# A decoder layer with 32 experts: the experts' last 32 slots on 512-wide column tiles, their later steps moved in the order

## The chip, the core and the metric

The kernel runs on one core of one Trainium2 chip. The metric is the device time of one execution in microseconds (us); the kernel before took 2203.43 us, the median of three runs (2196.72 to 2205.83). TensorE (PE) multiplies, VectorE (DVE) and ScalarE (ACT) work elementwise, GpSimd (POOL) issues the indirect transfers, and SyncE (SP) issues the loads of the weights. Each engine takes its instructions strictly in the order in which they stand in its program; only semaphores tie the engines together.

## The reference

One layer on 2048 tokens of width 1024, in float32: a mixer (gated linear attention beside dilated attention), then a hierarchical mixture of experts, then a norm. The change is in the experts alone:

```python
def hier_moe(n, w_grp, b_grp, w_exp, b_exp, w1, w3, w2):
    # top-1 group of 8 experts, then the top 2 experts in it; their gates
    gate = jax.nn.softmax(top_v, axis=-1) * g_prob
    ...
    def expert_block(args):
        toks, e = args
        xb = x[toks]
        hb = jax.nn.silu(xb @ w1[e]) * (xb @ w3[e])
        return hb @ w2[e]
    y = lax.map(expert_block, (row_tok.reshape(n_blk, MOE_BLOCK), blk_exp))
    y = y.reshape(R, D).astype(jnp.float32) * row_w[:, None]
    out = jnp.zeros((M, D), jnp.float32).at[row_tok].add(y)
```

There are 32 experts. `w1` and `w3` of an expert are 1024 x 512, `w2` is 512 x 1024. On average an expert gets 128 of the 4096 chosen places.

## The kernel before, in words

The program runs in stages: projections and linear attention, attention, output projection and router, and from about 1310 us on the experts, one after another (`moe`). A table made by the router gives each expert 160 slots. Slots 0 to 127 are an expert's **first rows**, slots 128 to 159 its **last 32 slots**. An overflow loop behind the experts takes what is left.

**Weights.** Each expert has six pieces of 1 MB, in the order w1a, w3a, w1b, w3b, w2a, w2b (L1319 to L1330). SyncE loads a piece into one of six buffers (`raw`), so a piece takes the buffer that the same piece of the expert before had, and its load waits until all readers of that one are done. ACT rounds it (`hi`), DVE subtracts (`lo`); the first rows use `hi` and `lo` in three products each, the last 32 slots read `raw` itself. So `raw` of w1 and w3 is free when the last 32 slots' first products have read it, and `raw` of w2 when their second products have.

**First rows of an expert.** U: 48 products of 128 x 512 (L1379 to L1381). Then `h` = silu times gate on ACT and DVE (L1393, L1394). X: four transposes (L1406). ACT and DVE copy them as `hh` and `hl` (L1409). D: 24 products with w2 (L1428 to L1430). ACT and DVE evict `y`, POOL adds it to the result in DRAM (L1436). T: eight transposes of the next expert's tokens (L1354) and their copies `nh` and `nl` (L1357).

**The last 32 slots.** Four products of 32 columns of the array stand beside each other, one on each quarter of it ("pack"). u: 32 products of 256 columns for w1 and w3 (L1388); `hr` = silu times gate (L1399, L1400); x: two transposes (L1414) and a copy `ht` (L1416); d: 16 products of 256 columns with w2 (L1444); one eviction `yr` (L1447) and an add (L1448).

**What sets the order.** The code records operations; a scheduler with its own costs then places each engine's instructions, so pieces of u stand between the products of U where it expected a wait. `behind` (NoSync) sets an order without a wait. `order` (called after expert 1) computes where every token's result goes, POOL scatters it in 16 transfers (L1251), and a load of `places` (L1256) reads it back on SyncE's queue. `entries` (called before expert 0) loads the table and computes the row numbers `i4` of the last slots' quarters on DVE (L1238 to L1240).

Of the kernel before, what the change touches and what calls it, by code (L numbers as in the profile page):

```python
# [60 lines left out]
class Layer:  # L61
# [1144 lines left out]
    def moe(self):  # L1206
        tc, nc, a = self.tc, self.nc, self.a
        with self.moest as st:
# [8 lines left out]
            rps = pool("e_rps", 2, space=PSUM)  # L1217
            acc4 = self.acc.rearrange("t (g c) -> (t g) c", g=4)
# [3 lines left out]
            i4A = keep.tile([128, NE], I32, name="i4")  # L1222
# [23 lines left out]
            def order():  # L1246
# [103 lines left out]

            def turn(G):
                tp = tps.tile([128, KD, 128], F32, name="tp")
                for k in range(KD):
                    nc.tensor.transpose(tp[:, k, :], G[:, k * 128:(k + 1) * 128], self.ident)  # L1354
# [13 lines left out]
            def up(w, x, nr=None):  # L1368
# [25 lines left out]
                nc.vector.tensor_tensor(to(h), by(ps[1]), to(h), OP.mult)  # L1394
                hr = None
                if nr is not None:
                    hr = gp.tile([128, 256], F32, name="hr", bufs=1)
                    by, to = (lambda t: t.rearrange("t (p k) -> t k p", k=2)), hr[64:128].rearrange("t (k p) -> t k p", k=2)
                    nc.scalar.activation(to, by(pr[0:64]), AF.Silu)  # L1399
                    nc.vector.tensor_tensor(to, by(pr[64:128]), to, OP.mult)  # L1400
                return h, hr

            def across(h, hr):
                tp = mm.tile([128, 4, 128], F32, name="mm")
                for k in range(4):
                    nc.tensor.transpose(tp[:, k, :], h[:, k * 128:(k + 1) * 128], self.ident)  # L1406
# [3 lines left out]
                ht = None  # L1410
                if hr is not None:
                    tr = rps.tile([128, 2, 64], F32, name="r")
                    for c in range(2):
                        nc.tensor.transpose(tr[:, c, :], hr[64:128, c * 128:(c + 1) * 128], self.ident[64:128, 64:128])  # L1414
                    ht = gp.tile([128, 2, 2, 32], F32, name="ht", bufs=1)
                    nc.vector.tensor_copy(ht, tr.rearrange("p c (u s) -> p u c s", u=2))  # L1416
                return hh, hl, ht

            def down(w2, x, it, irs, e=None):
                hh, hl, ht = x  # L1420
                y = yp.tile([128, D], F32, name="y", bufs=1)
                gate = it[:, 1:2].bitcast(F32)
                for f in range(2):
                    py = mm.tile([128, 512], F32, name="mm")
                    fs = slice(f * 512, (f + 1) * 512)
                    for k in range(4):
                        raw, hi, lo = w2[k // 2]
                        nc.tensor.matmul(py, hh[:, k, :], hi[:, k % 2, fs], start=k == 0, stop=False)  # L1428
# [4 lines left out]
                    else:  # L1433
# [3 lines left out]
                                                   in_=y, in_offset=None, compute_op=OP.add), e)  # L1437
                if ht is not None:
                    ir, i4 = irs
                    pr = rps.tile([128, 256], F32, name="r")  # L1440
# [7 lines left out]
                    added(nc.gpsimd.indirect_dma_start(out=acc4, out_offset=bass.IndirectOffsetOnAxis(ap=i4, axis=0),  # L1448
                                                       in_=yr, in_offset=None, compute_op=OP.add), e)
# [15 lines left out]
            for e in range(NE):  # L1465
# [7 lines left out]
                if e % 4 == 0 and e + 2 < NE:  # L1473
                    R = gather_last(e // 4, min(4, NE - 2 - e))
                h = across(*up((w1, w3), x, nr[:, :, at:at + 32]))
                at += 32
                if e + 1 < NE:
                    x = turn(G.pop(e + 1))
                    if e % 4 == 1:
                        nr, at = turn_last(R, 32 * min(4, NE - 1 - e)), 0  # L1480
                    for t, c in zip(self.turned, self.crossed):
                        self.behind(t, c, "what the tensor engine waits for comes first")
                if e == 0:
                    self.firstst.close()
                    yp = pool("e_y", 1)
                if e == NE - 1:

                    done = [(j, x, scale(x, self.crossed)) for j, x, _ in blocks]
                    for d in done[0:2]:
                        give(*d, after=(self.crossed[1],))  # L1490
                down(w2, h, itA[:, e], (irA[:, e], i4A[:, e:e + 1]), e)
                if waiting:
# [14 lines left out]
            with tc.For_i(0, n, 1) as i:  # L1507
# [10 lines left out]
                x = turn(gx)  # L1518
                down(w2, across(*up((w1, w3), x)), it, None)
                m = nc.values_load(cur[:, 2:3], min_val=0, max_val=NT)  # L1520
# [96 lines left out]
```

## Time and profile before

| What | Value |
|---|---|
| median of three runs | 2203.43 us |
| the profiled execution | 2199.59 us, its span 2197.6 us |
| mean granted TensorE clock over the span | 0.971 |
| PE busy, DVE, ACT, POOL | 2081.0, 1273.2, 1057.4, 529.7 us |
| experts, first X to last X | 1341.2 to 2153.7 us |
| DMA, HBM read and written | 342.46 MB and 92.08 MB |

A row of a timeline gives start, duration, engine, line, operation, `out<-in` and shape; instructions of one group that follow each other are merged (x64 is 64 records; a float32 product of u or d leaves two records). In brackets stands the idle time of the engine before the row, and what ended it. A busy PE counts records that overlap, so the distance between starts is what a product costs.

### The profile page before, as it was taken

To read this page: it belongs to the slowest core of one execution; us is meant where nothing else is said; L and a number is where in the kernel's file an instruction comes from. 1 tells how busy PE (TensorE), PEld (TensorE's weight loads), DVE (VectorE), ACT (ScalarE), POOL (GpSimd) and SP (SyncE) were. 2 spreads that over 40 slices of the span, in tenths; PEclk is the share of its full clock that TensorE was granted. 3 is DMA by queue.
4 is the path that set the end of the run, shared out by engine and by line. 5 is a ranking of instruction groups with operands and counts; after the bars stand their busy time and mean duration, and the time that the engine had idled before them with its cause. 6 is when DMAs were issued, how large, how long until landed. Compare 5 with 4: busy or idle time off the path is not lost. (4 is left out here: it accounts for less than half of the span.)

```text
span 2197.6 us, 38549 instructions
## 1 busy us (share of the span) xinstructions
PE 2081.0 (95%) x15258; PEld 1564.8 (71%) x15258; DVE 1273.2 (58%) x2481; ACT 1057.4 (48%) x1813; POOL 529.7 (24%) x370
## 2 busy tenths in 40 slices
PE   7999999999997999999989968999999999999993
PEld 7799889899885766666667755667677666667662
DVE  5203346334444556666645875767777677776773
ACT  5412336433322367767723443555555555565652
POOL 2000001000002001432421243622232254333334
PEclk9999999999998999999989979999999999999997
DMA  8333333233325624552457836788888889898974
GB/s 253 107 125 106 114 113 121 96 110 123 105 87 171 199 75 125 152 135 81 115 161 254 272 129 209 265 290 302 303 305 295 284 304 354 309 340 290 345 280 140
DMA packets 189000, 436.56 MB, mean 199 GB/s; under 512 B 35025, under 2 KB 106498, under 8 KB 162946
## 3 DMA queue, kind: packets, MB, share of 16 engines
q1 hardware_dynamic: 139090, 347.65, 44.9%
q0 software_dynamic: 21488, 60.36, 10.3%
q10 hardware_dynamic: 28240, 26.07, 4.0%
q8 instruction: 121, 1.98, 0.4%
q14 instruction: 61, 0.50, 0.1%
HBM read 342.46 MB, written 92.08 MB: 198 GB/s over the span
## 5 line engine op out<-in xcount | busy, mean ns | idle before, releaser
L1329 DVE TENSOR_TENSOR lo<-raw,hi 128x2048 fp32r<-128x2048 f32 x192 | 438.5, 2290 | 122.5 <-ACT hi L1329 121.3
L1329 ACT CAST hi<-raw 128x2048 fp32r<-128x2048 f32 x192 | 365.0, 1905 | 194.7 <-DMA raw<-expert_w 163.1
L588 ACT ACTIVATE P<-P,st 128x256 f32<-128x256 f32 (+1 forms) x384 | 174.0, 455 | 96.6 <-DVE st L586 92.2
L1381 PE MATMUL mm<-lo,nh 128*128 128x512 f32 x512 | 206.2, 404 | 0.7 <-DVE lo L1329 0.7
L1379 PE MATMUL mm<-hi,nh 128*128 128x512 f32 x512 | 204.4, 400 | 1.3 <-ACT nh L1357 1.3
L1380 PE MATMUL mm<-hi,nl 128*128 128x512 f32 x512 | 201.4, 393 | 0.0
L131 POOL TENSOR_TENSOR ss<-ss,mhalf 128x1 f32<-128x1 f32 (+1 forms) x32 | 28.9, 903 | 692.9 <-DVE ss L130 691.4
L217 PE MATMUL mm<-whi,nh 128*128 128x256 f32 x640 | 182.3, 285 | 0.0
L218 PE MATMUL mm<-wlo,nh 128*128 128x256 f32 x640 | 180.6, 282 | 0.0
L219 PE MATMUL mm<-whi,nl 128*128 128x256 f32 x640 | 179.5, 280 | 0.0
L586 DVE CUSTOM_DVE_ANT_0 P<-s,amask 128x256 f32<-128x256 f32 (+1 forms) x384 | 125.0, 362 | 66.4 <-PE s L582 42.9
L194 PE MATMUL mm<-nh,whi 128*128 128x512 f32 x384 | 155.3, 404 | 0.0
L195 PE MATMUL mm<-nl,whi 128*128 128x512 f32 x384 | 153.8, 400 | 0.0
L196 PE MATMUL mm<-nh,wlo 128*128 128x512 f32 x384 | 152.7, 398 | 0.0
L1388 PE MATMUL r<-raw,nr 128*32 128x256 f32 x2048 | 147.1, 383 | 0.0
L582 PE MATMUL s<-k,q 64*128 64x256 f32 (+1 forms) x768 | 132.8, 416 | 0.4 <-DVE st L586 0.4
L1381 PEld LDWEIGHTS mm<-lo,nh 128*128 128x128 f32 x512 | 96.6, 189 | 41.0 <-issue 17.3
L1436 POOL DMA_INDIRECT acc<-y,it x32 | 84.7, 2647 | 155.9 <-ACT y L1432 147.0
L185 DVE TENSOR_TENSOR wlo<-raw,whi 128x1024 fp32r<-128x1024 f32 (+1 forms) x48 | 57.1, 1227 | 111.4 <-ACT whi L184 111.4
L217 PEld LDWEIGHTS mm<-whi,nh 128*128 128x128 f32 x640 | 120.0, 188 | 2.0 <-issue 0.7
L219 PEld LDWEIGHTS mm<-whi,nl 128*128 128x128 f32 x640 | 121.1, 189 | 0.1
L218 PEld LDWEIGHTS mm<-wlo,nh 128*128 128x128 f32 x640 | 120.3, 188 | 0.1
(352 smaller groups left out, 4412.3 us busy)
## 6 DMA issues: line engine op xcount, KB each, us to landing
raw<-expert_w SPq DMA_DIRECT2D x192, 1024.0 KB, 9.6
raw<-w_in ACTq DMA_DIRECT2D x48, 512.0 KB, 5.0
fb<-fac SPq DMA_DIRECT2D x24, 384.0 KB, 7.7
x<-x SPq DMA_DIRECT2D x16, 512.0 KB, 6.2
og<-og SPq DMA_DIRECT2D x32, 256.0 KB, 2.9
xr<-x SPq DMA_DIRECT2D x32, 256.0 KB, 3.0
v<-av SPq DMA_DIRECT2D x8, 1024.0 KB, 7.9
hp<-xr SPq DMA_DIRECT2D x32, 256.0 KB, 2.2
```

The lines of the kernel that those rows point to most:

```text
L194: nc.tensor.matmul(ps, hi[:, k, ms], nh[q][:, k, :], start=k == 0, stop=False)
L195: nc.tensor.matmul(ps, hi[:, k, ms], nl[q][:, k, :], start=False, stop=False)
L196: nc.tensor.matmul(ps, lo[:, k, ms], nh[q][:, k, :], start=False, stop=k == KD - 1)
L217: nc.tensor.matmul(ps[:, j, :], h, hi[:, k, :], start=j == 0 and k == 0, stop=False, skip_group_check=True)
L218: nc.tensor.matmul(ps[:, j, :], h, lo[:, k, :], start=False, stop=False, skip_group_check=True)
L219: nc.tensor.matmul(ps[:, j, :], l, hi[:, k, :], start=False, stop=k == KD - 1, skip_group_check=True)
L588: nc.scalar.activation(P[:, h, 0:w], P[:, h, 0:w], AF.Exp, bias=nm, scale=-1.0, accum_out=dn)
L1329: split = nc.scalar.copy(hi, raw), nc.vector.tensor_tensor(lo, raw, hi.bitcast(F32), OP.subtract)
L1379: nc.tensor.matmul(ps[m], nh[:, k, :], hi[:, kk, :], start=k == 0, stop=False)
L1380: nc.tensor.matmul(ps[m], nl[:, k, :], hi[:, kk, :], start=False, stop=False)
L1381: nc.tensor.matmul(ps[m], nh[:, k, :], lo[:, kk, :], start=False, stop=k == KD - 1)
L1388: nc.tensor.matmul(pr[32 * g:32 * g + 32], nr[:, k, :], raw[:, k % 4, (g % 2) * 256:(g % 2) * 256 + 256], start=k == 0, stop=k == KD - 1, ...
```

## The change

Five things change; the code around them stays.

- u and d use 512-wide products, half as many: two quarters of the array take w1 and w3 of one part of the contraction, the other two those of another part. Their results are halves of a sum that must be added: ACT copies one half and DVE adds the other (`sm`), silu and gate follow on 32 x 512 (`sg`, `hr`); after d, ACT scales one half and DVE adds the other (`yr`). Row numbers are now of half rows (`i2`).
- `gated` is recorded after T and its copies, and is put behind them on ACT and DVE (`self.ahead`).
- x is recorded inside the second half of D instead of before D, d stays behind D.
- T is put behind X (`turn(..., self.inner)`).
- The row numbers of the last slots are computed behind `hl` of expert 0 (`rows`), and the load of `places` comes after expert 4 (`order_late`).

```diff
@@ entries, order
-                f4 = gp.tile([128, NE], F32, name="f4", bufs=1)
-                nc.vector.tensor_copy(f4[:, es], irA[:, es, 0])
-                nc.vector.tensor_scalar(f4[:, es], f4[:, es], 4.0, self.gcol, OP.mult, OP.add)
-                nc.vector.tensor_copy(i4A[:, es], f4[:, es])
+            def rows(es):
+
+                f2 = gp.tile([64, NE], F32, name="f2", bufs=1)
+                self.behind(nc.vector.tensor_copy(f2[:, es], irA[0:64, es, 0]), self.crossed[1], "the table's entries come later than the first inner values")
...
+                return free, sts
+
+            def order_late(free, sts):
                 l = nc.sync.dma_start(places, self.perm.rearrange("(p j) c -> p (j c)", p=128))
@@ up
-                    pr = rps.tile([128, 256], F32, name="r")
-                    for k in range(KD):
+                    pr = rps.tile([128, 512], F32, name="r")
+                    for k in range(0, KD, 2):
                         for g in range(4):
-                            raw = w[g // 2][k // 4][0]
-                            nc.tensor.matmul(pr[32 * g:32 * g + 32], nr[:, k, :], raw[:, k % 4, (g % 2) * 256:(g % 2) * 256 + 256],
-                                             start=k == 0, stop=k == KD - 1, skip_group_check=True, tile_position=(0, 32 * g))
+                            kk, raw = k + g // 2, w[g % 2][k // 4][0]
+                            nc.tensor.matmul(pr[32 * g:32 * g + 32], nr[:, kk, :], raw[:, kk % 4, :],
+                                             start=k == 0, stop=k == KD - 2, skip_group_check=True, tile_position=(0, 32 * g))
...
+            def gated(pr):
+
+                hr = gp.tile([128, 256], F32, name="hr", bufs=1)
+                sm = gp.tile([64, 512], F32, name="sm", bufs=1)
+                sg = gp.tile([64, 512], F32, name="sg", bufs=1)
+                first = nc.scalar.copy(sm, pr[64:128]), nc.vector.tensor_tensor(sm, pr[0:64], sm, OP.add)
+                for f, t in zip(first, self.ahead):
+                    self.behind(f, t, "the wide products come first")
+                act = nc.scalar.activation(sg[32:64], sm[0:32], AF.Silu)
+                by = lambda t, u: t[:, 256 * u:256 * u + 256].rearrange("t (p k) -> t k p", k=2)
+                for u in range(2):
+                    to = hr[64 + 32 * u:96 + 32 * u].rearrange("t (k p) -> t k p", k=2)
+                    vec = nc.vector.tensor_tensor(to, by(sm[32:64], u), by(sg[32:64], u), OP.mult)
+                self.gated = act, vec
+                return hr
@@ down
+                        if f and k == 2 and hr is not None:
+                            ht = across_last(hr)
...
-                    for k in range(4):
+                    for k in range(0, 4, 2):
...
-                            nc.tensor.matmul(pr[32 * g:32 * g + 32], ht[:, k // 2, k % 2, :], raw[:, k % 2, g * 256:g * 256 + 256],
-                                             start=k == 0, stop=k == 3, skip_group_check=True, tile_position=(0, 32 * g))
-                    yr = yp.tile([128, 256], F32, name="yr", bufs=1)
-                    nc.vector.tensor_scalar(yr, pr, ir[:, 1:2].bitcast(F32), None, OP.mult)
+                            kk, f = g // 2, g % 2
+                            nc.tensor.matmul(pr[32 * g:32 * g + 32], ht[:, k // 2, kk, :], raw[:, kk, f * 512:f * 512 + 512],
+                                             start=k == 0, stop=k == 2, skip_group_check=True, tile_position=(0, 32 * g))
+                    yr = yp.tile([64, 512], F32, name="yr", bufs=1)
+                    nc.scalar.activation(yr, pr[64:128], AF.Copy, scale=ir[64:128, 1:2].bitcast(F32))
+                    nc.vector.scalar_tensor_tensor(yr, pr[0:64], ir[0:64, 1:2].bitcast(F32), yr, op0=OP.mult, op1=OP.add)
@@ the loop over the experts
-                h = across(*up((w1, w3), x, nr[:, :, at:at + 32]))
+                h, pr = up((w1, w3), x, nr[:, :, at:at + 32])
+                h = across(h)
                 at += 32
+                self.ahead = self.crossed
                 if e + 1 < NE:
-                    x = turn(G.pop(e + 1))
+                    x = turn(G.pop(e + 1), self.inner)
...
+                    rows(slice(0, NE))
...
+                hr = gated(pr)
...
-                down(w2, h, itA[:, e], (irA[:, e], i4A[:, e:e + 1]), e)
+                down(w2, h, itA[:, e], hr, (irA[:, e], i2A[:, e:e + 1]), e)
...
-                    order()
+                    ordered = order()
+                if e == 4:
+                    order_late(*ordered)
```

What the scheduler makes of it is read from the built programs. First TensorE around the second pack (d), a middle expert of the kernel before: T, x, D, d, then the next expert's U, with u in three pieces between its products and X at the end.

```order
L1354 MATMUL tp<-ident,G 128x128 x8
L1414 MATMUL r<-ident,hr 128x64 x2
L1428 MATMUL mm<-hi,hh 128x512 x2
...
L1444 MATMUL r<-raw,ht 32x256 x16
L1379 MATMUL mm<-hi,nh 128x512
...
L1388 MATMUL r<-raw,nr 32x256 x5
...
L1388 MATMUL r<-raw,nr 32x256 x23
L1406 MATMUL mm<-ident,h 128x128 x4
```

The same stretch of a middle expert of the changed kernel: D (L1449 to L1451) is followed by U of the next expert (L1386 to L1388), and x (L1433) and d (L1466) stand between those products.

```order
L1359 MATMUL tp<-ident,G 128x128 x8
L1449 MATMUL mm<-hi,hh 128x512 x2
...
L1386 MATMUL mm<-hi,nh 128x512
...
L1433 MATMUL r<-ident,hr 128x64 x2
...
L1466 MATMUL r<-raw,ht 32x512 x8
L1396 MATMUL r<-raw,nr 32x512 x16
L1424 MATMUL mm<-ident,h 128x128 x4
```

x has left the place between T and D, and d has moved from the end of D to behind all 48 of the next expert's U, just ahead of u and X.

Then DVE at expert 0 before (`nr` is the copy of the last slots' transposed tokens, `f` and `i` the row numbers, `lo` a piece's subtraction):

```order
L1365 COPY nr<-tp 128x8x64
L1238 CAST f_13075<-ir 128x32
L1239 TENSOR_SCALAR f_13075<-f_13075,kcol 128x32
L1329 TENSOR_TENSOR lo<-raw,hi 128x2048
L1240 CAST i_13038<-f_13075 128x32
L1394 TENSOR_TENSOR h<-mm,h 128x512
```

and in the changed kernel:

```order
L1372 COPY nr<-tp 128x8x64
L1334 TENSOR_TENSOR lo<-raw,hi 128x2048
L1402 TENSOR_TENSOR h<-mm,h 128x512
L1427 TENSOR_TENSOR hl<-mm,hh 128x512
L1240 CAST f_13207<-ir 64x32
L1241 TENSOR_SCALAR f_13207<-f_13207,kcol 64x32
L1242 CAST i_13038<-f_13207 64x32
```

The row numbers, which read the table's entries, now stand behind `h` and `hl` of expert 0.

## Rows read from the trace of the kernel before

**Rows 1.** The page's busy line: engine, us, share of the span, instructions.
```profile
PE 2081.0 (95%) x15258; PEld 1564.8 (71%) x15258; DVE 1273.2 (58%) x2481; ACT 1057.4 (48%) x1813; POOL 529.7 (24%) x370
```
**Rows 2.** Window over the experts: us, busy (x) PE, PEld, DVE, ACT, POOL, PEclk, DMA, GB/s.
```profile
1450.00:2150.00 700.00, 692.45 (x4967) 482.96 (x4960) 501.30 (x380) 401.89 (x319) 241.69 (x117) 1.00 0.87 308
```
**Rows 3.** Timeline of PE, the first X (expert 0) and the last (expert 31).
```profile
1341.20 1.12 PE L1406 MATMUL mm<-ident,h 128*128 128x128 f32 x4 [7.97 <-DVE h L1394]
...
2153.65 0.66 PE L1406 MATMUL mm<-ident,h 128*128 128x128 f32 x4
```
**Rows 4.** Timeline of PE, one expert's turn: start us, us, engine, line.
```profile
1809.59 3.66 PE L1388 MATMUL r<-raw,nr 128*32 128x256 f32 x64
1813.18 0.65 PE L1406 MATMUL mm<-ident,h 128*128 128x128 f32 x4
1813.67 1.04 PE L1354 MATMUL tp<-ident,G 128*128 128x128 f32 x8
1814.64 0.33 PE L1414 MATMUL r<-ident,hr 64*128 64x64 f32 x2
1814.90 0.73 PE L1428 MATMUL mm<-hi,hh 128*128 128x512 f32 x2
...
1820.68 1.93 PE L1444 MATMUL r<-raw,ht 128*32 128x256 f32 x32
```
**Rows 5.** Timeline of PE, a piece of u between two products of U.
```profile
1826.35 0.39 PE L1379 MATMUL mm<-hi,nh 128*128 128x512 f32 x1
1826.57 0.39 PE L1380 MATMUL mm<-hi,nl 128*128 128x512 f32 x1
1826.89 1.05 PE L1388 MATMUL r<-raw,nr 128*32 128x256 f32 x10
1827.87 0.50 PE L1381 MATMUL mm<-lo,nh 128*128 128x512 f32 x1
```
**Rows 6.** Waits of SyncE's queue, 1450 to 2150 us: total us, times, longest.
```profile
SPq L1324 <- PE r L1388: 430.0, 55, 19.4
SPq L1324 <- PE r L1444: 175.3, 54, 11.6
```
**Rows 7.** Weight loads' landing: all from 1400 us, then pairs issued at 1631, 1591.
```profile
DMA to landing us min/median/max: 4.8/9.8/17.2
...
DMA to landing us min/median/max: 4.8/5.8/6.8
...
DMA to landing us min/median/max: 5.6/7.7/9.8
```
**Rows 8.** Groups by line: busy us, mean ns, idle us before and what ended it.
```profile
L1329 DVE TENSOR_TENSOR lo<-raw,hi 128x2048 fp32r<-128x2048 f32 x192 | 438.5, 2290 | 122.5 <-ACT hi L1329 121.3
L1329 ACT CAST hi<-raw 128x2048 fp32r<-128x2048 f32 x192 | 365.0, 1905 | 194.7 <-DMA raw<-expert_w 163.1
...
L1409 DVE TENSOR_TENSOR hl<-mm,hh 128x512 fp32r<-128x512 f32 x32 | 22.1, 691 | 7.2 <-ACT hh L1409 6.7
...
L1393 ACT ACTIVATE h<-mm 128x512 f32<-128x512 f32 x32 | 19.0, 595 | 38.8 <-PE mm L1381 38.8
...
L1447 DVE TENSOR_SCALAR yr<-r,ir 128x256 f32<-128x256 f32 x32 | 15.3, 479 | 9.6 <-PE r L1444 5.0 <-PE mm L1430 4.6
...
L1400 DVE TENSOR_TENSOR hr<-r,hr 64x256 f32<-64x256 f32 x32 | 13.7, 427 | 24.2 <-ACT hr L1399 23.9
```
**Rows 9.** Timeline of DVE at expert 0, idle time before it in brackets.
```profile
1337.81 0.18 DVE L1238 CAST f<-ir 128x32 f32<-128x32 int32 x1 [14.96 <-DMA ir<-table]
```
**Rows 10.** Timeline of DVE and of PE at expert 3.
```profile
1424.33 0.17 DVE L1261 TENSOR_SCALAR pf<-places 128x16 f32<-128x16 int32 x1 [6.03 <-DMA places<-perm]
...
1425.16 0.66 PE L1406 MATMUL mm<-ident,h 128*128 128x128 f32 x4 [2.59 <-DVE h L1394]
```
**Rows 11.** Windows just after that wait (columns as in rows 2).
```profile
1425.00:1428.00 3.00, 2.76 (x23) 1.68 (x27) 2.31 (x7) 2.15 (x3) 0.99 (x1) 0.87 1.02 333
1428.00:1432.00 4.00, 4.00 (x34) 2.11 (x27) 2.90 (x2) 1.15 (x1) 0.00 (x0) 0.67 1.03 318
```

More of the change, by code (lines that the diff above doesn't have):

```diff
@@ L1217, in moe @@
             rps = pool("e_rps", 2, space=PSUM)
-            acc4 = self.acc.rearrange("t (g c) -> (t g) c", g=4)
+            acc2 = self.acc.rearrange("t (g c) -> (t g) c", g=2)
             table = self.table.rearrange("(e r) c -> r e c", e=NE)
@@ L1221, in moe @@
             irA = keep.tile([128, NE, 2], I32, name="ir")
-            i4A = keep.tile([128, NE], I32, name="i4")
+            i2A = keep.tile([64, NE], I32, name="i2")
             irG = keep.tile([128, NE // 4, 2], I32, name="irg")
@@ L1349, in gather_last, with turn @@
                 return R
-            def turn(G):
+            def turn(G, after=None):
                 tp = tps.tile([128, KD, 128], F32, name="tp")
                 for k in range(KD):
-                    nc.tensor.transpose(tp[:, k, :], G[:, k * 128:(k + 1) * 128], self.ident)
+                    t = nc.tensor.transpose(tp[:, k, :], G[:, k * 128:(k + 1) * 128], self.ident)
+                    if after is not None:
+                        self.behind(t, after, "these cover the copies of the inner values")
                 nh = gp.tile([128, KD, 128], F32R, name="nh")
@@ L1394, in up, with across @@
                 nc.vector.tensor_tensor(to(h), by(ps[1]), to(h), OP.mult)
[L1395 to L1403, printed above, removed]
+                return h, pr
+            def gated(pr):
[12 more added lines that the diff above has]
+                return hr
+            def across(h):
                 tp = mm.tile([128, 4, 128], F32, name="mm")
                 for k in range(4):
-                    nc.tensor.transpose(tp[:, k, :], h[:, k * 128:(k + 1) * 128], self.ident)
+                    self.inner = nc.tensor.transpose(tp[:, k, :], h[:, k * 128:(k + 1) * 128], self.ident)
                 hh = gp.tile([128, 4, 128], F32R, name="hh", bufs=1)
@@ L1409, in across, with across_last, down @@
                 self.crossed = nc.scalar.copy(hh, tp), nc.vector.tensor_tensor(hl, tp, hh.bitcast(F32), OP.subtract)
[L1410 to L1420, printed above, removed]
+                return hh, hl
+            def across_last(hr):
+                tr = rps.tile([128, 2, 64], F32, name="r")
+                for c in range(2):
+                    nc.tensor.transpose(tr[:, c, :], hr[64:128, c * 128:(c + 1) * 128], self.ident[64:128, 64:128])
+                ht = gp.tile([128, 2, 2, 32], F32, name="ht", bufs=1)
+                nc.vector.tensor_copy(ht, tr.rearrange("p c (u s) -> p u c s", u=2))
+                return ht
+            def down(w2, x, it, hr=None, irs=None, e=None):
+                hh, hl = x
                 y = yp.tile([128, D], F32, name="y", bufs=1)
@@ L1437, in down @@
                                                    in_=y, in_offset=None, compute_op=OP.add), e)
-                if ht is not None:
-                    ir, i4 = irs
-                    pr = rps.tile([128, 256], F32, name="r")
-                    for k in range(4):
+                if hr is not None:
+                    ir, i2 = irs
+                    pr = rps.tile([128, 512], F32, name="r")
+                    for k in range(0, 4, 2):
                         raw = w2[k // 2][0]
                         for g in range(4):
-                            nc.tensor.matmul(pr[32 * g:32 * g + 32], ht[:, k // 2, k % 2, :], raw[:, k % 2, g * 256:g * 256 + 256],
-                                             start=k == 0, stop=k == 3, skip_group_check=True, tile_position=(0, 32 * g))
-                    yr = yp.tile([128, 256], F32, name="yr", bufs=1)
-                    nc.vector.tensor_scalar(yr, pr, ir[:, 1:2].bitcast(F32), None, OP.mult)
-                    added(nc.gpsimd.indirect_dma_start(out=acc4, out_offset=bass.IndirectOffsetOnAxis(ap=i4, axis=0),
+                            kk, f = g // 2, g % 2
[4 more added lines that the diff above has]
+                    nc.vector.scalar_tensor_tensor(yr, pr[0:64], ir[0:64, 1:2].bitcast(F32), yr, op0=OP.mult, op1=OP.add)
+                    added(nc.gpsimd.indirect_dma_start(out=acc2, out_offset=bass.IndirectOffsetOnAxis(ap=i2, axis=0),
                                                        in_=yr, in_offset=None, compute_op=OP.add), e)
@@ L1474, in moe @@
                     R = gather_last(e // 4, min(4, NE - 2 - e))
-                h = across(*up((w1, w3), x, nr[:, :, at:at + 32]))
+                h, pr = up((w1, w3), x, nr[:, :, at:at + 32])
+                h = across(h)
                 at += 32
+                self.ahead = self.crossed
                 if e + 1 < NE:
-                    x = turn(G.pop(e + 1))
+                    x = turn(G.pop(e + 1), self.inner)
                     if e % 4 == 1:
                         nr, at = turn_last(R, 32 * min(4, NE - 1 - e)), 0
+                    self.ahead = self.turned
                     for t, c in zip(self.turned, self.crossed):
@@ L1483, in moe @@
                 if e == 0:
+                    rows(slice(0, NE))
                     self.firstst.close()
                     yp = pool("e_y", 1)
+                hr = gated(pr)
                 if e == NE - 1:
-                    done = [(j, x, scale(x, self.crossed)) for j, x, _ in blocks]
+                    done = [(j, x, scale(x, self.gated)) for j, x, _ in blocks]
                     for d in done[0:2]:
-                        give(*d, after=(self.crossed[1],))
-                down(w2, h, itA[:, e], (irA[:, e], i4A[:, e:e + 1]), e)
+                        give(*d, after=(self.gated[1],))
+                down(w2, h, itA[:, e], hr, (irA[:, e], i2A[:, e:e + 1]), e)
                 if waiting:
@@ L1518, in moe @@
                 x = turn(gx)
-                down(w2, across(*up((w1, w3), x)), it, None)
+                down(w2, across(up((w1, w3), x)[0]), it)
                 m = nc.values_load(cur[:, 2:3], min_val=0, max_val=NT)
```

2 lines of the change are left out of this document (added).

## The prediction

> **What bounds the kernel now.** I read the page first: PE is busy 95% of the span, no other engine over 58% [rows 1]. The window over the experts says the same, sharper: 692 of 700 us on PE at a granted clock of 1.00, DVE 501, ACT 402, DMA engines 87% [rows 2]. So a term counts in the experts only if it stands in PE's program or makes PE wait. From the first X to the last are 812.5 us, 31 turns of 26.2 us [rows 3].
>
> The timeline of one turn gives its parts [rows 4]: u unbroken 3.59 us (start to start), X 0.49, T 0.97, x 0.26, D 5.78, d 1.93. U is 48 products at 0.22 to 0.23 [rows 5], so 10.9. Sum 23.9. The missing 2.3 us are mostly pieces of u between the products of U: such a piece of 10 records takes 0.98 where ten of the unbroken 64 take 0.56, and is entered 0.1 later than a product would be [rows 5]; 0.5 us a piece.
>
> Then the queue that loads the weights, since d moves and d is what it waits for. SyncE waits 430 us for u and 175 us, 54 times, for d [rows 6]: the two pieces of w2 of expert e+1 lie in the buffers of expert e's, which d reads last. Here d starts 5.8 us after D does [rows 4], some 20 us ahead of the next D, so this wait costs PE nothing. How long the way from a freed buffer to PE is: a load lands 4.8 us after its issue at the least, 9.8 in the median of 170, which wait for each other too. Of a pair issued together when the queue was empty the first landed after 4.8 and the second after 6.8; of a w2 pair, beside an expert's additions into DRAM, after 5.6 and 9.8 [rows 7]. ACT then rounds a piece in 1.9 us and DVE subtracts in 2.3; hl, which most of D needs, takes DVE 0.7 [rows 8].
>
> **The change, part by part.** The sum is against the profiled execution's own 2199.6 us; the median shown is 3.8 above it.
>
> Wider products. u issues 16 products of 512 columns in place of 32 of 256, d 8 in place of 16: the same columns in all. The trace has no such product. If a set of four cost the same as now, u and d would halve (gain 2.7 us a turn); if it costs twice, nothing is gained. The nearest rows are a transpose of 128 columns (T, 0.97/8 = 0.12) and a set of four records of 256 columns (3.59/16 = 0.224) [rows 4]: time grows with the columns, 0.10 for each 128, so 512 cost about 0.43. I take a gain of 0.2 us a turn: -7.
>
> Pieces. Counted in the two programs, u stands in 61 pieces instead of 102, d in 32 instead of 39. At 0.5 us that is up to -24; but a broken set is now twice as wide, and eight of the new turns break u into three or four pieces. I take -4.
>
> Expert 0. DVE's copy of the row numbers waits 15 us for the table [rows 9], with h queued behind it, and PE idles 8.0 us [rows 3]. The copy moves behind hl: -8, or nothing if expert 1's pieces, loaded after the same table, are late in its place. I take -8.
>
> Places. At expert 3 DVE waits 6.0 us for the load of places, and PE 2.6 for the h behind it [rows 10]; after expert 4 the scatters have long landed: -2.6. After that idle stretch the granted clock was 0.87 for 3 us and 0.67 for 4 [rows 11], which loses 0.4 + 1.3 = 1.7 us; with the like after expert 0, -3. All gains: 25 us.
>
> More elementwise work. DVE gets sm (near the 0.69 of hl), two hr (0.43 each, where there was one) and a yr of 0.7 for 0.48; ACT two copies and a wider silu near 0.6 each [rows 8]: 1.3 us more a turn on either. DVE is at 18.8 of 26.2 us [rows 2]: it lies beside PE, unless on the way below.
>
> The later d. After the change d stands behind 26 to 48 of the next expert's U. In 15 of 31 turns nothing but at most five U, u, X and T is left between d and the next D ("late"); in 8 a piece of u, ten U and the rest of u ("middle"); in 8 some 22 U and all of u ("early"). For each, the way of the w2 pieces against PE's own work:
> - Late. The first piece is free after half of d (0.9), lands 5.6 later, is rounded (1.9) and subtracted (2.3), then hl (0.7): 11.4 us, 10.6 with the shortest load. PE has d 1.9, one U 0.3, u 3.6, X 0.5, T 1.0 and the two products that need hh alone 0.5: 7.7. PE waits 3.7 us (least 2.9).
> - Middle. Here DVE's program has both subtractions ahead of hl. The second piece lands 2.2 after the first: 0.9 + 5.6 + 2.2 + 1.9 + 2.3 + 0.7 = 13.6 (least 12.8; 16.6 if it lands 9.8 after its issue). PE has 1.9 + 1.9 + 2.3 + 2.8 + 2.0 = 10.8. Wait 2.8 (2.0 to 5.8).
> - Early. PE has 1.9 + 5.0 + 4.9 + 2.0 = 13.8 against the same 13.6: no wait (to 2.8).
>
> I take 5.6, of the pair that is the same pieces; its 9.8 has an addition beside it that now comes some 10 us before d. Waits: 15 x 3.7 + 8 x 2.8 = 78. Least: 15 x 2.9 + 8 x 2.0 = 60. With loads of 9.8: 15 x 7.9 + 8 x 5.8 + 8 x 2.8 = 187.
>
> The clock after such waits: 2.6 us of idle PE lost 1.7 us [rows 10, 11], against none seen in the experts' window. I count 0.85 (half of it) for the 15 late ones: +13.
>
> By the Trainium skill (DMA: Bandwidth & Descriptors, Bandwidth) a transfer of 1 MB takes 6.15 us; here two lone ones took 4.8 and 5.6 [rows 7], so the measurements decide; by the page the waits would be 23 x 0.55 = 13 us more.
>
> Sum: 78 + 13 - 25 = +66; on the median 2203.4 that is 2270.
>
> **Rivals.** *The wait is covered (faster).* PE idles only 7.5 of 700 us [rows 2] although ACT waited 163 us for loads [rows 8]: loads here are late to ACT without hurting PE. If the w2 pieces are in time, only the gains stand: 2203 - 25 = 2178. Against it: in a late turn the load would have to land 1.9 us after its issue, and none of 170 took less than 4.8. It decides from a mean wait of under 0.8 us a turn.
> *They cancel.* A mean wait of 0.8 us (25/31), from early turns being commoner in effect than the program shows: 2203.
> *The clock falls at every wait.* 23 waits x 1.7 = 39 in place of 13, beside second loads at 9.8 in the middle turns (8 x 3.0 = 24): 2270 + 26 + 24 = 2320. For it: the drop was seen after 2.6 us [rows 11]; its granted 0.67 is a mixture of the two levels, 2.4 and 1.2 GHz. Against it: D's first two products break a wait in two. The Trainium skill (TensorE: Matmul & The Clock Gate, HAM oscillation) says that idle gaps between bursts bring the half clock back each time; rows 11 agree for one gap.
> *Width pays.* If 512 columns cost a set what 256 do, 83 us come back and the late d costs the same: about 2195; the growth from 128 to 256 columns speaks against it.
>
> **How the numbers follow.** Less than 0.5% (11 us) can't be told from no change. Forecast (2215 to 2300) 0.60; clock and slow loads (over 2300) 0.19; covered 0.10 and width 0.04, both faster in the main; cancelled 0.07, in it all within 11 us. So faster 0.13, same 0.07, slower 0.80. The range leaves out most of the covered case and a little above: 2198 to 2330; the forecast's own is 2215 to 2300.
>
> **What would show it.** PE idle before D's products with DVE's hl or lo as releaser, 2 to 5 us in turns whose d stands just before u; SyncE's wait for d grown from 175 us to several hundred, and stretches of some 10 us without weight loads; X to X near 28 us instead of 26.2; no 15 us wait of DVE at expert 0 and X about 8 us earlier there; u unbroken still near 3.6 us. Wrong it would be if D follows T without idle in the late turns, if u takes near 1.8 us, or if the loads land under 3 us.

## The result and the profile after

The changed kernel takes 2314.95 us (median, 2310.23 to 2316.88) against 2202.76 for the kernel before: ratio 1.0512, 95% interval 1.0492 to 1.0533. It is 112 us slower; the forecast was 67 us slower, in a range of 2198 to 2330. The result lies in that range, but above the 2215 to 2300 of the forecast's own case. The place and the mechanism were those forecast, one price in the sum was far too low.

Windows over the same 700 us as in [rows 2] and from the first X to the last (columns as there):

```profile
1450.00:2150.00 700.00, 625.81 (x3215) 404.56 (x3208) 464.79 (x378) 386.35 (x325) 176.46 (x104) 0.95 0.77 273
...
1327.00:2260.00 933.00, 833.22 (x4226) 535.53 (x4222) 612.20 (x515) 503.94 (x424) 250.11 (x149) 0.94 0.76 265
```

PE's idle time in the 700 us went from 7.5 to 74.2 us and the granted clock from 1.00 to 0.95. The first and the last X, which answer to [rows 3]:

```profile
1327.29 0.66 PE L1424 MATMUL mm<-ident,h 128*128 128x128 f32 x4
...
2260.20 0.66 PE L1424 MATMUL mm<-ident,h 128*128 128x128 f32 x4 [0.90 <-DVE h L1402]
```

31 turns take 932.9 us, 30.1 each, in place of 26.2. PE's groups by line from the first X to the last (busy, mean ns, idle before and what ended it) say where the idle time stands:

```profile
L1386 PE MATMUL mm<-hi,nh 128*128 128x512 f32 x496 | 199.8, 403 | 13.4 <-ACT hi L1334 12.6 <-ACT nh L1364 0.8
L1450 PE MATMUL mm<-hi,hl 128*128 128x512 f32 x248 | 116.4, 471 | 41.2 <-DVE hl L1427 41.0
L1451 PE MATMUL mm<-lo,hh 128*128 128x512 f32 x248 | 108.4, 448 | 1.4 <-DVE lo L1334 1.4
L1449 PE MATMUL mm<-hi,hh 128*128 128x512 f32 x248 | 107.4, 453 | 35.3 <-ACT hh L1427 34.5 <-ACT hi L1334 0.7
```

D waits 35.3 + 41.2 + 1.4 = 78 us, nearly all of it for hh and for hl. U waits 13.4 us for `hi` and, by its third product (L1388), 5.2 us for `lo`; in the kernel before it waited 0.9 us. One late turn, in timelines of PE, SyncE, ACT and DVE, shows the whole way:

```profile
1746.17 1.92 PE L1466 MATMUL r<-raw,ht 128*32 128x512 f32 x16
1747.91 3.62 PE L1396 MATMUL r<-raw,nr 128*32 128x512 f32 x32
1751.46 0.65 PE L1424 MATMUL mm<-ident,h 128*128 128x128 f32 x4
1751.95 1.04 PE L1359 MATMUL tp<-ident,G 128*128 128x128 f32 x8
1754.73 0.73 PE L1449 MATMUL mm<-hi,hh 128*128 128x512 f32 x2 [1.74 <-ACT hh L1427]
1757.05 0.79 PE L1450 MATMUL mm<-hi,hl 128*128 128x512 f32 x1 [1.58 <-DVE hl L1427]
1757.64 0.63 PE L1451 MATMUL mm<-lo,hh 128*128 128x512 f32 x1
1758.07 0.63 PE L1449 MATMUL mm<-hi,hh 128*128 128x512 f32 x1
```
```profile
1747.30 5.10 SPq L1329 DMA_DIRECT2D raw<-expert_w  x6
```
```profile
1752.17 1.90 ACT L1334 CAST hi<-raw 128x2048 fp32r<-128x2048 f32 x1 [3.32 <-DMA raw<-expert_w]
1754.09 0.58 ACT L1427 CAST hh<-mm 128x512 fp32r<-128x512 f32 x1
```
```profile
1754.10 2.29 DVE L1334 TENSOR_TENSOR lo<-raw,hi 128x2048 fp32r<-128x2048 f32 x1 [4.48 <-ACT hi L1334]
1756.31 0.68 DVE L1427 TENSOR_TENSOR hl<-mm,hh 128x512 fp32r<-128x512 f32 x1
```

d starts at 1746.17; its first half frees the buffer and SyncE issues the load at 1747.30; ACT has the data at 1752.17, 4.9 us later. ACT's program has `hi` of that piece ahead of `hh`, DVE's has `lo` ahead of `hl`, so both copies of the inner values, which X delivered at 1752, wait for a weight. PE has d, u, X and T to do (6.8 us) and then idles 1.74 and 1.58. The last two rows of PE show a second price: D's products now follow each other at 0.43 us instead of 0.23. The window there, and SyncE's waits (1450 to 2150 us, as [rows 6]):

```profile
1756.00:1762.00 6.00, 4.95 (x12) 3.89 (x13) 6.00 (x6) 4.94 (x5) 0.00 (x0) 0.50 1.02 421
```
```profile
SPq L1329 <- PE r L1466: 479.2, 48, 25.6
```

The clock granted is 0.50, the lower level, 1.2 GHz. A mean of 0.94 over 933 us is 56 us lost; in the window above PE was busy 4.95 of 6.00 us, so by this estimate some 46 us of the loss fall on products. The half clock does not follow every wait: in windows from X to X the clock is below 1.00 in 20 of the 31 turns and 1.00 in 11, of which ten have 1.0 to 3.9 us of idle time. One of these ten:

```profile
1633.69:1663.47 29.78, 25.92 (x139) 16.10 (x135) 19.61 (x16) 17.77 (x14) 5.33 (x3) 1.00 0.79 277
```

The sum between first and last X: 932.9 - 812.4 = 120.5 us. Of these 89 are idle time (99.8 in place of 10.9, the latter from the row below). About 42 are the clock: the 46, less the 4 that the kernel before lost in two turns at 0.93 and 0.94. About -10 is left for the products themselves. The first X comes 13.9 us earlier and the end is 4 us longer: 111, the difference of the two spans.

```profile
1341.00:2154.00 813.00, 802.14 (x5713) 558.28 (x5714) 579.02 (x452) 459.15 (x363) 294.67 (x148) 1.00 0.85 302
```

### The profile page after: what moved, and what is told of

Its sections match the earlier page's. It is cut to its first block, busy times and chain, and to the rows that moved or that the text cites. A ratio compares the mean times of both kernels' runs of the same rounds, so it can differ in the third digit from the quotient of the medians.

```text
span 2308.5 us, 35639 instructions
## 1 busy us (share of the span) xinstructions
PE 2108.1 (91%) x13722; PEld 1538.7 (67%) x13722; DVE 1309.6 (57%) x2545; ACT 1105.3 (48%) x1877; POOL 484.0 (21%) x370
## 5 line engine op out<-in xcount | busy, mean ns | idle before, releaser
L1386 PE MATMUL mm<-hi,nh 128*128 128x512 f32 x512 | 207.2, 405 | 14.5 <-ACT hi L1334 12.6
L1388 PE MATMUL mm<-lo,nh 128*128 128x512 f32 x512 | 205.5, 406 | 5.2 <-DVE lo L1334 5.1
L1450 PE MATMUL mm<-hi,hl 128*128 128x512 f32 x256 | 120.2, 471 | 42.9 <-DVE hl L1427 42.8
L1449 PE MATMUL mm<-hi,hh 128*128 128x512 f32 x256 | 111.0, 454 | 36.9 <-ACT hh L1427 36.2
L1396 PE MATMUL r<-raw,nr 128*32 128x512 f32 x1024 | 138.6, 595 | 0.0
L1388 PEld LDWEIGHTS mm<-lo,nh 128*128 128x128 f32 x512 | 97.8, 191 | 50.5 <-issue 10.9
L1386 PEld LDWEIGHTS mm<-hi,nh 128*128 128x128 f32 x512 | 98.2, 192 | 45.2 <-ACT hi L1334 16.1
```

The costliest lines, as they stand in the source:

```text
L1386: nc.tensor.matmul(ps[m], nh[:, k, :], hi[:, kk, :], start=k == 0, stop=False)
L1388: nc.tensor.matmul(ps[m], nh[:, k, :], lo[:, kk, :], start=False, stop=k == KD - 1)
L1396: nc.tensor.matmul(pr[32 * g:32 * g + 32], nr[:, kk, :], raw[:, kk % 4, :], start=k == 0, stop=k == KD - 2, skip_group_check=True, tile_po ...
```

## The experiments

The changed kernel put x and d late, made the pack of 512 columns, and moved two small things. The first three runs ask which of these moves d; the next three what an early d or a free buffer gives; then the clock, the copies, and the small parts. Each ratio is to the kernel before in the same runs (its medians there: 2201.1, 2206.8 and 2205.0 us).

### What moves d: the width of u

wide_u: the kernel before with u alone wide, recorded where it was.

```diff
-                    pr = rps.tile([128, 256], F32, name="r")
...
+                    pr = rps.tile([128, 512], F32, name="r")
...
-                    nc.scalar.activation(to, by(pr[0:64]), AF.Silu)
-                    nc.vector.tensor_tensor(to, by(pr[64:128]), to, OP.mult)
...
+                    nc.scalar.copy(sm, pr[64:128])
+                    nc.vector.tensor_tensor(sm, pr[0:64], sm, OP.add)
+                    nc.scalar.activation(sg[32:64], sm[0:32], AF.Silu)
...
```

> The kernel before, with u alone 512 columns wide, its halves added as in the changed kernel, but recorded where hr was before; d, x, T, the row numbers and places as before. The order that comes of it has x and d 20 to 38 products of U behind D all the same, and u whole. Theory (the longer way from u to hr moves x and d back, and the late d makes D wait): 10 to 20 products of U lie between d and the next u, so PE has 10 to 12 us against the w2 pieces' 10.8 (the way seen in the changed kernel: 1.1 + 4.8 + 1.9 + 2.3 + 0.6): waits of 0 to 2.5 us in a turn and stretches at half clock, less some 30 us for u in 34 pieces in place of 102: 2200 to 2270 us, idle time ahead of and inside D 20 to 60 us. Rival (what is recorded later in the changed kernel moves d, not the width): no wait for D, 2170 to 2190 us.

2351.74 us, ratio 1.0652 (1.0632 to 1.0672): slower than the whole change, and above the 2270 expected. PE's idle time ahead of D, by line:

```profile
L1435 PE MATMUL mm<-hi,hl 128*128 128x512 f32 x248 | 124.5, 502 | 40.1 <-DVE hl L1415 40.0
L1434 PE MATMUL mm<-hi,hh 128*128 128x512 f32 x248 | 118.2, 498 | 85.9 <-ACT hh L1415 85.7
```

126 us of waits for hh and hl, at a clock of 0.91 over the experts: the width of u with the longer way to hr that it needs moves x and d back and brings the loss, although u stands in 33 pieces in place of some 102. No run has the one without the other. D follows X directly in most turns here, so nothing covers the wait; in the change T stands between them. That T took some of the wait there is likely, but no run shows it alone.

wide_d: the same for d alone (`pr` 512 wide, `yr` of two halves).

> The kernel before, with d alone 512 columns wide, its halves scaled and added as in the changed kernel. x and d stay just ahead of or behind D in the order; u stands in 136 pieces in place of 102. Theory: no wait for D comes of it (less than 10 us idle ahead of and inside D), the products of 512 columns cost what two of 256 do (a set of four 0.43 us), and 34 more pieces at 0.5 us make 17 us: 2205 to 2225 us. Rival (the width and the two evictions of yr cost by themselves): D waits and the time is above 2240.

2230.4 us, ratio 1.0116 (1.0101 to 1.0130); D idles 6 us. The excess, 24 us, is near the 17 counted for 34 more pieces of u. The width of d makes no wait.

u_narrow: the changed kernel with u at 256 columns and hr of one silu and one product; d stays wide.

> The changed kernel with u 256 columns wide again, and with hr of one silu and one product as before; all else of the change stays (d wide, x recorded inside D, hr behind T's copies, T behind X, the row numbers, places). In its order x and d stand behind 24 to 26 products of the next expert's U, but the rest of U and three or four pieces of u follow them. Theory (u's width and the way to hr carry the loss): PE has 13 us or more between d and the next D, and the w2 pieces' way is 10.8 to 13: idle time ahead of and inside D below 30 us in place of 76, granted clock over the experts 0.97 or more, 2200 to 2250 us. Rival (that d stands behind U at all is enough): within 20 us of the changed kernel, 2295 to 2335.

2266.56 us, ratio 1.0286 (1.0259 to 1.0313), above the range expected. D still waits 46 us:

```profile
L1443 PE MATMUL mm<-hi,hl 128*128 128x512 f32 x248 | 105.9, 427 | 29.0 <-DVE hl L1420 29.0
L1442 PE MATMUL mm<-hi,hh 128*128 128x512 f32 x248 | 99.5, 422 | 16.5 <-ACT hh L1420 15.7 <-issue 0.8
```

So going back to the narrow u gives 48 of the 112 us, though u stands in more pieces again (93, in place of some 60). D's waits are the larger part of what is left: even with a quick hr, x stands right behind D and d behind some 26 products of U in most turns. That the late recording keeps d there is likely, but no run changes it alone.

### What an early d and a free buffer give

d_first: the changed kernel, d ahead of the next U by order alone.

```diff
...
+                            if k == 0 and nr is not None and self.second is not None:
+                                self.behind(first, self.second, "the second pack frees the weights")
...
```

> The changed kernel, with the next expert's first products U put behind d (an order, no wait), so that the order is T, D, x, d, U, u, X in every turn. If the late place of d is what costs (theory: d frees the w2 buffers some 10 us before D instead of 20), the idle PE ahead of and inside D (36 and 41 us between the first X and the last) goes, and the half clock with it (0.94 to about 1.00). A turn is then 10.9 + 3.6 + 0.5 + 1.0 + 5.8 + 0.3 + 1.9 + 0.4 for changes between kinds = 24.4 us of products. U may wait instead: u, now whole at the turn's end, frees w1a and w3a about 11 us before U's third product, and the way of a piece is 5 to 7 + 1.9 + 2.3 us: 0 to 2.6 us a turn. 31 turns of 24.4 to 27.0 in place of 30.1: 2140 to 2220 us. Rival 1 (the wide products and the sum of their halves cost it): x and d then wait for hr, and the time stays above 2280.

2343.05 us, ratio 1.0646 (1.0623 to 1.0668). The theory's wait went and the time did not: PE by line, then one turn on PE and DVE.

```profile
L1468 PE MATMUL r<-raw,ht 128*32 128x512 f32 x496 | 109.5, 1031 | 79.4 <-issue 38.8 <-ACT hi L1334 29.7 <-ACT junk L1288 10.8
L1452 PE MATMUL mm<-hi,hl 128*128 128x512 f32 x248 | 100.4, 405 | 0.0
...
L1451 PE MATMUL mm<-hi,hh 128*128 128x512 f32 x248 | 96.0, 408 | 0.0
...
L1435 PE MATMUL r<-ident,hr 64*128 64x64 f32 x62 | 11.1, 262 | 58.6 <-DVE hr L1419 58.6
```
```profile
1721.11 0.33 PE L1435 MATMUL r<-ident,hr 64*128 64x64 f32 x2 [1.43 <-DVE hr L1419]
1723.68 3.64 PE L1468 MATMUL r<-raw,ht 128*32 128x512 f32 x16 [2.23 <-ACT hi L1334]
```
```profile
1717.89 2.28 DVE L1334 TENSOR_TENSOR lo<-raw,hi 128x2048 fp32r<-128x2048 f32 x1
1720.20 0.85 DVE L1419 TENSOR_TENSOR hr<-sm,sg 32x256 f32<-32x256 f32 x2
1721.08 2.29 DVE L1334 TENSOR_TENSOR lo<-raw,hi 128x2048 fp32r<-128x2048 f32 x1
1723.29 0.28 DVE L1437 COPY ht<-r 128x128 f32<-128x128 f32 x1
```

D waits 0.0, so the late place of d did cause D's waits. But x now waits for hr, behind a subtraction, and d for the copy ht, behind another. For d's wait the profile names ACT's `hi`, which the DVE rows correct: ht ends at 1723.57 and d starts at 1723.68. 138 us of idle time replace 78, with the clock at 0.89.

d_first_u_narrow: the same with u at 256 columns.

> As u_narrow, with the next expert's U put behind d as in d_first: T, D, x, d, U, u, X. In d_first PE idled 1.4 us ahead of x and 2.2 ahead of d in nearly every turn, since the sum, the silu and two products of hr stand between subtractions of weights on DVE. With a silu and one product x should have hr in time (hr is then done some 3 us earlier). Theory (the longer way to hr cost d_first its gain): the idle ahead of x goes, that ahead of d shrinks below 1 us where the copy of ht has no subtraction ahead of it, the clock returns to 0.97 or more: 2190 to 2240 us. Rival (the copy of ht behind the subtractions keeps d waiting 2 us or more whatever hr needs): 2270 us or more.

2329.03 us, ratio 1.0577 (1.0548 to 1.0606): the rival held.

```profile
L1461 PE MATMUL r<-raw,ht 128*32 128x512 f32 x496 | 97.5, 925 | 129.3 <-issue 82.2 <-ACT hi L1334 33.9 <-ACT junk L1288 13.2
```

x waits 0.0 us now, and d 129 us. One turn on PE and DVE shows for what: x ends at 1718.77, and the copy ht stands behind an eviction of y and a subtraction. The profile names no releaser there ("issue"), but ht ends at 1721.93 and d starts at 1722.03.

```profile
1718.44 0.33 PE L1428 MATMUL r<-ident,hr 64*128 64x64 f32 x2
1722.03 2.79 PE L1461 MATMUL r<-raw,ht 128*32 128x512 f32 x12 [3.26 <-issue]
```
```profile
1719.45 2.28 DVE L1334 TENSOR_TENSOR lo<-raw,hi 128x2048 fp32r<-128x2048 f32 x1
1721.65 0.28 DVE L1430 COPY ht<-r 128x128 f32<-128x128 f32 x1
```

So x's place behind D costs, and not only hr's length: ahead of D, as before and in the last run below, the copy lies beside D.

d_other: the changed kernel with d reading a constant tile in place of w2; the values of the last 32 slots are left out.

```diff
...
-                            nc.tensor.matmul(pr[32 * g:32 * g + 32], ht[:, k // 2, kk, :], raw[:, kk, f * 512:f * 512 + 512],
+                            nc.tensor.matmul(pr[32 * g:32 * g + 32], ht[:, k // 2, kk, :], fg[:, f * 512:f * 512 + 512],
...
```

> The changed kernel, with the second products d reading a constant tile of the same width in place of w2 (the values of the last 32 slots are left out by this; count, width and place of the products stay, and d stands as late as in the changed kernel or later). Nothing then holds the w2 buffers but the rounding and the subtraction. Theory (the buffers that d holds): the idle time ahead of and inside D, 76 us, goes nearly wholly, and the clock returns to 0.98 to 1.00: 2315 - 76 - 40 = about 2200, 2180 to 2220. Rival 2 (hh and hl stand behind the rounding and the subtraction of w2 in the programs of ACT and DVE, and the loads are late for other reasons, such as the additions into DRAM): the waits stay and the time is above 2290.

2256.03 us, ratio 1.0252 (1.0233 to 1.0271): half of the loss goes, but D's waits do not, against the theory.

```profile
L1449 PE MATMUL mm<-hi,hl 128*128 128x512 f32 x248 | 111.4, 449 | 39.6 <-DVE hl L1426 39.6
...
L1448 PE MATMUL mm<-hi,hh 128*128 128x512 f32 x248 | 105.5, 446 | 35.8 <-ACT hh L1426 35.7
```

The sum of the waits is nearly the same, 75 us in place of 78, but they are other ones: 26 us stand at experts 0 and 3 (15.3 and 10.2 there), where the new order put weights ahead of hh. In the other turns D waits some 50 us in place of 78, although in nearly all of them d stands just ahead of u, as in the late turns. SyncE no longer waits for d, but 122 us for `lo` on DVE. Part of what was gained is not d's at all: the new order has u in 31 pieces, the changed kernel in some 60. So waits of this kind come without d's hold on the buffers too, and what the hold costs this run does not show.

### The clock

fill: the changed kernel with 341 products of no use where PE idled.

```diff
...
+                    for n in range(5):
+                        t = nc.tensor.matmul(pys[0], self.spare[:, 0, :], self.spare[:, 0:4, :], start=True, stop=True)
...
+                            for n in range(6):
+                                t = nc.tensor.matmul(pys[1], self.spare[:, 0, :], self.spare[:, 0:4, :], start=True, stop=True)
...
```

> The changed kernel with 5 more products of 512 columns (1.1 us) between T and D and 6 (1.4 us) behind the first product of D, in places where PE idles 1.2 and 1.4 us a turn; their results are overwritten by D's own first products. Theory (idle stretches of PE bring the half clock, and that costs some 47 us): the granted clock over the experts rises from 0.94 to 0.98 or more, and the time falls by 20 to 45 us to 2270 to 2295, though 341 products were added. Rival 3 (the clock falls by something else than idle PE, or costs less): the clock stays at 0.94, and the time stays or grows by up to 20 us where the products are longer than the wait.

2321.22 us, ratio 1.0541 (1.0514 to 1.0569), the changed kernel's time. The window over the experts:

```profile
1336.00:2279.00 943.00, 877.26 (x4565) 577.69 (x4564) 612.46 (x515) 504.61 (x425) 238.01 (x150) 0.98 0.76 262
```

The clock rose from 0.94 to 0.98 as expected: the idle stretches bring the half clock. The time did not fall: from the first X to the last it grew by 10 us (942.9 for 932.9), though 77 us of products (341 of 0.227) took the place of only 34 us of idle time (65.7 are left of 99.8). So 77 - 34 - 10 = 33 us came back with the clock, near the 38 that 0.04 of 943 us are: the clock's price is of the size said, but it can't be bought back in this way.

### Weights ahead of the copies

d_first_u_split (as d_first, u's first half ahead of U's second) and early_two (the kernel before with the small parts below, u in two pieces) both free w1a and w3a early (early_two's lines):

```diff
...
+                            if k == 3 and g == 3:
+                                for s in second:
+                                    self.behind(s, t, "the first half's weights go first")
...
```

> As d_first, and the first half of u (8 products, with w1a and w3a) stands ahead of U's second half: U24, u8, U24, u8, X in every turn. The two buffers that U needs first are free some 7 us earlier, for 0.5 to 0.7 us a turn of one more piece of u. If in d_first U waits for w1a and w3a, this kernel is the faster: 31 turns of 25.0 us, 2150 to 2180 us. If U does not wait there, it is slower than d_first by 15 to 22 us.

> As early, and u (256 wide) in two pieces by order alone: 16 products behind U's first half, 16 behind its second. 38 fewer pieces at 0.5 us are 19 us less: 2175 us (2165 to 2185) if nothing else moves. Rival: w1a and w3a then come free earlier, and their rounding and subtraction are put ahead of hh and hl in the programs of ACT and DVE, as in d_first_u_split, where PE idled 120 us ahead of and inside D: above 2230 us.

d_first_u_split takes 2430.95 us (ratio 1.1036, 1.1008 to 1.1065), with 120 us of waits for hh and hl. Neither branch of its expectation held: U had waited 0.0 us in d_first, so 15 to 22 us more than d_first were due, and it is 88 more. early_two takes 2358.79 us (1.0696, 1.0676 to 1.0715) and goes by its rival, which was taken from d_first_u_split. Its ACT and PE at one expert:

```profile
1507.22 1.90 ACT L1333 CAST hi<-raw 128x2048 fp32r<-128x2048 f32 x1 [0.58 <-DMA raw<-expert_w]
1509.14 0.38 ACT L1417 ACTIVATE hr<-r 64x256 f32<-64x256 f32 x1
1509.55 0.59 ACT L1427 CAST hh<-mm 128x512 fp32r<-128x512 f32 x1
```
```profile
1505.92 0.60 PE L1424 MATMUL mm<-ident,h 128*128 128x128 f32 x4
...
1510.18 0.73 PE L1446 MATMUL mm<-hi,hh 128*128 128x512 f32 x2 [3.34 <-ACT hh L1427]
```

X is done at 1506.5, but ACT's program has a piece that lands at 1507.2 ahead of hr and hh: hh starts 3 us after X, and D waits 3.34 us, with d near its old place. That is the same wait as in the changed kernel, without its cause.

### The small parts, and a faster kernel

early: the row numbers and places alone.

> The kernel before with two parts of the change alone: the row numbers of the last slots behind hl of expert 0, and the load of places after expert 4. From the changed kernel's trace: its X of expert 0 came 13.9 us earlier, but that of expert 1 only 4.9, since PE then idled 7.8 us behind D of expert 0; the wait of 2.6 us at expert 3 goes, with 3.5 us of products at half clock (1.7 us). Theory: 2203 - 4.9 - 4.3 = 2194 us, 2190 to 2199. Rival (expert 1's weights, loaded behind the same table, take all of it): within 3 us of the kernel before.

2202.17 us, ratio 0.9980 (0.9965 to 0.9996): a gain of 4.6 us, half of the 9 expected, and less than the 0.5% that counts here. early_cover adds T behind X:

> As early (the kernel before with the row numbers behind hl of expert 0 and places after expert 4), and T behind X in every turn, as in the changed kernel. All turns then have the order of the kernel before's quickest ones (25.1 to 25.3 us), in place of a third of them at 26 to 27. Theory: D's first products lose no cover and u has 7 pieces less; 31 turns of 25.6 instead of 26.4 us in early: 2180 us (2170 to 2195). Rival (T ahead of X covered a wait for the weights there): 2200 us or more.

2209.14 us, ratio 1.0017 (1.0002 to 1.0031): no gain, against 2180 expected; the rival held. From X to X, 12 of the 31 turns take 25.1 to 25.2 us, like the quickest before. The others, among them those with a D cut by U and those with u in four to six pieces, take more, most of them 26 to 29. early_cover_whole_u adds an order of u behind U:

```diff
...
+                            if k == 0 and g == 0:
+                                for s in self.wide:
+                                    self.behind(t, s, "u comes whole")
...
```

> As early_cover, with u (256 wide) behind all of U: T, x, D, d, U, u, X. 63 pieces less at 0.5 us are 31 us. But u's first half frees w1a and w3a 10.8 us before U, whose third product needs w1a loaded (4.8 to 7), rounded (1.9) and subtracted (2.3): 9.0 to 11.2, more where DVE has other work between. Theory (such a wait comes in every turn and brings the half clock): U waits 1 to 3 us a turn, 2220 to 2290 us. Rival (the pieces weigh more): U waits less than 0.5 us and the time is 2150 to 2175 us.

2176.39 us, ratio 0.9866 (0.9846 to 0.9886), 1.3% below the kernel before: the theory fell, the rival held (U waits 0.4 us a turn; its range was missed by 1 us). A turn, and the window over the experts:

```profile
1526.85 0.66 PE L1417 MATMUL mm<-ident,h 128*128 128x128 f32 x4
...
1528.31 0.33 PE L1425 MATMUL r<-ident,hr 64*128 64x64 f32 x2
1528.57 0.73 PE L1439 MATMUL mm<-hi,hh 128*128 128x512 f32 x2
...
1534.26 1.93 PE L1455 MATMUL r<-raw,ht 128*32 128x256 f32 x32
...
1547.22 3.66 PE L1396 MATMUL r<-raw,nr 128*32 128x256 f32 x64
1550.81 0.44 PE L1417 MATMUL mm<-ident,h 128*128 128x128 f32 x2
```
```profile
1336.00:2130.00 794.00, 765.30 (x5716) 559.69 (x5713) 579.48 (x454) 462.41 (x364) 297.40 (x150) 0.99 0.88 312
```

This turn takes 24.0 us from X to X with no idle time, the sum of the parts in [rows 4, 5]: x ahead of D, d right behind it, u whole, the 256 columns kept.

## Why the prediction was right, and where its size was off

- *The late d.* The step was right: D waits for hh and hl behind the late w2 pieces. The way in the late turn above is 1.1 + 4.9 + 1.9 + 2.3 + 0.6 = 10.8 us from the start of d to hl's end at 1756.99, against 11.4 forecast; the load is 0.7 shorter than the 5.6 taken, nearer the least. (The prediction calls the 4.8 and 5.6 lone loads; by [rows 7] they are the first loads of two pairs.) The sum, 78 us forecast and 78 measured, agrees by luck. The wait that followed was 3.1 us on average after the 15 late turns (3.7 forecast, least 2.9), 2.9 after the 8 middle ones (2.8) and 1.2 after the early ones (counted at 0, with up to 2.8): 46, 23 and 9 us in place of 56, 22 and 0.
- *The clock.* This term was mis-sized: "I count 0.85 (half of it) for the 15 late ones: +13". About 46 us were lost, in 20 turns, some 2.3 us in each. In the late turn the wait brought 0.50 over several us of D, where products follow each other at 0.43 us in place of 0.23; `fill` shows that the idle time is the cause. The result lies in the case of the rival "the clock falls at every wait", which had 0.19. Its 39 us for the clock were the better price, but its other half did not come: the middle turns waited 2.9 us and not 5.8, so that its 2320 was near by luck. The Trainium skill (TensorE: Matmul & The Clock Gate, HAM oscillation) describes a kernel whose gaps between bursts bring the half clock back each time. The trace agrees in 20 turns and not in the ten others that idled 1.0 to 3.9 us at 1.00; what decides between them no run here shows.
- *Idle time ahead of U.* The sum had no term for it. U waits 18.6 us in place of 0.9, half of it at the first three experts.
- *Wider products.* -7 was wrong: u unbroken takes from 1747.91 to 1751.46, 3.55 us, against 3.59 [rows 4]. 512 columns cost twice what 256 do.
- *Pieces.* -4 was too careful: with -7 it makes -11, and the -10 left for all products, which carries the error of the clock's estimate, is then nearly all the pieces'. Whole, u gives more: 33 us between early_cover and early_cover_whole_u for 63 pieces, 0.5 each as read from [rows 5].
- *Expert 0.* The 15 us wait of DVE went and X came 13.9 us earlier, not 8; but the condition named held, expert 1's pieces are late in its place (PE idles 5.30 and 2.51 us behind D of expert 0, both for `hi`), and X of expert 1 comes only 4.9 us earlier. With places, `early` measures 4.6 us for both, not 8 + 3 + 3.
- *What would show it.* SyncE's wait for d rose from 175 to 479 us, as said; X to X became 30.1 and not 28, in the main by the clock and by U's waits.
- *The rivals.* "The wait is covered" and "They cancel" needed a mean wait of under or near 0.8 us a turn; it was 2.5. "Width pays" needed u near 1.8 us; it took 3.55.

Open: how much of the 112 us is d's hold on the buffers alone. d_other changed the order with it, and a kernel with more than six buffers was not tried. Open too is how the loss divides between u's width and the sum of its halves.

## What to carry to other kernels

An instruction that frees a buffer is part of the path of whatever is loaded there next: before moving it later, count from its new end through the load and the elementwise steps to the first reader. Where weights and results share an engine's strict order, a late weight holds the results queued behind it; look at what stands ahead of the copy that the bottleneck waits for. And a wait that comes back in most turns can cost more than its length, through the clock: here 100 us of idle time, 78 of it ahead of D, lost about 46 more.

## What the runs showed of the hardware

The pack's cost grows with its columns: a set of four products takes 0.224 us at 256 columns and 0.44 at 512 (3.55 us for 8 sets by the starts, where 16 sets took 3.59). Breaking u out between U's products costs some 0.5 us a piece and shows in no idle time: with 63 pieces less 33 us went, while PE's idle time grew from 22 to 29 us. Short waits that recur lower the clock, but not each of them: with 100 us of idle time spread over 31 turns the granted mean was 0.94 (20 turns below 1.00, ten others at 1.00 in spite of 1.0 to 3.9 us of idle time), with 143 us (d_first) 0.89, and with 29 us (early_cover_whole_u) 0.99.
